# Transposing a stack of 32x32 blocks as one compact 128-partition tile, with ScalarE gathering and scattering

## The chip, the cores and the metric

The kernel runs on one core of a Trainium2 chip. The metric is the device time of one execution in microseconds (us). The time before is the median of three runs, 3059.33 us (3055.2 to 3061.43).

## The reference

A decoder trunk of two layers (SEQ 1024, D_MODEL 1024, float32). Each layer projects the input, runs three kinds of heads side by side (4 stick-breaking attention heads, 4 latent attention heads, 8 RWKV-7 heads), adds the result through a layer norm, and ends with a gated convolutional feed-forward block. The part that matters here is the recurrence of the RWKV-7 heads:

```python
def step(state, inp):
    r_t, w_t, k_t, v_t, kk_t, a_t = inp
    sa = jnp.einsum('bhvk,bhk->bhv', state, -kk_t)
    state = (state * w_t[:, :, None, :] + sa[..., None] * (kk_t * a_t)[:, :, None, :]
             + v_t[..., None] * k_t[:, :, None, :])
    return state, jnp.einsum('bhvk,bhk->bhv', state, r_t)
```

The kernel does not run it token by token. It cuts the 1024 tokens into 16 chunks of 64. Inside a chunk, each token's `sa` depends on the earlier tokens of the chunk through a strictly triangular 64x64 matrix, so that every chunk of every head needs the inverse of (identity minus that matrix).

## The kernel before, in words

The program is one long list of instructions per engine. The engines are TensorE (PE), VectorE (DVE), ScalarE (ACT), GpSimd (POOL), and SyncE (SP), which issues every DMA. A scheduler has put the instructions of all stages in one order, by priorities and by its own model of the durations. Each engine then runs its own list strictly in that order, and waits at an instruction whose inputs are not ready while everything behind it waits too.

Each of the two layers has these stages: projections and preparation of the RWKV heads (`proj_rw`, `rw_prep`, `rw_stage1`), the inversion (`rw_inv`), the walk over the chunks (`rw_chain`), the two kinds of attention, the output projection, and the feed-forward block. `rw_inv` runs twice in a layer (`st` 0 and 1, four heads each), so four times in the program. It is a generator: `phase_a` advances it between projections (`step`), so that its instructions lie among those of other stages. The first inversion of a layer lies among the projections, preparation and `rw_stage1` of the next heads; the second lies among the chunk walk of the first four heads and the projections of stick-breaking attention.

One call of `rw_inv` inverts 64 matrices of 64x64. `Aa` holds them: four heads by 16 chunks in the free dimension, two chunks side by side in the partition halves. The diagonal 32x32 blocks are first transposed into `LA` (line 725, four instructions of 32 partitions each, one per group of 32 partitions). VectorE inverts them by forward substitution, many small multiplications (line 729, product into the scratch tile `pd`) and sums (line 730, result into `T`). `T` is then transposed as a whole into `LA` (line 750, a tile of 128 partitions), TensorE forms the products with the off-diagonal blocks (line 759, evicted by ScalarE at line 762 into the buffer of `pd`), GpSimd clears the whole of `Aa` (line 764), and VectorE transposes `T` back into the diagonal blocks of `Aa`, now called `Z` (line 767, four instructions of 32 partitions). TensorE makes the off-diagonal block of the inverse (line 776, evicted at 779) and applies the inverse to `xt` (line 788, evicted at 789). `xt` is loaded from DRAM by SyncE (line 784) into the buffers of `LA` and `T`, and stored to `psd` (line 792), from which `rw_chain` loads it (line 831).

`LA`, `T` and `pd` have one buffer each: a new tile of a name waits until every reader of the old one is done.

Names that the text uses around it: `psmm` are the projections' matrix products (lines 205 to 207, 24 for each half of 512 tokens); lines 596 and 597 are two matmuls that sum over a head, whose inputs come from ScalarE (line 200) and VectorE (line 201); lines 844 to 847 make the matrices `QC` of the chunk walk (matmul, VectorE additions, ScalarE copy); lines 863 and 866 carry its state.

Of the kernel before, what the change touches and what calls it, by code (L numbers as in the profile page):

```python
# [17 lines left out]
P = 128  # L18
S = 1024
# [50 lines left out]
class Body:  # L70
# [640 lines left out]
    def rw_inv(self, st, tp, Aa):  # L711
        nc = self.nc
        v32 = lambda t: t.rearrange("p (a b) -> p a b", b=32)
        LA = v32(self.t(tp, [P, S], "LA"))
        T = v32(self.t(tp, [P, S], "T"))
        pd = self.t(tp, [P, S], "pd")
        M = self.t(tp, [P, 16, 16], "M")
        nc.gpsimd.memset(T, 0.0)
        Tf = T.rearrange("p a b -> p (a b)")
        nc.gpsimd.memset(Tf[:, 0:1024:33], 1.0)  # L720
        Af = Aa.rearrange("p h (j e) x -> p (h j) e x", e=2)
        for q in range(4):
            r = slice(32 * q, 32 * q + 32)
            x0 = 32 * (q % 2)
            nc.vector.transpose(LA[r], Af[r, :, q // 2, x0 : x0 + 32].rearrange("p f t -> p t f"))  # L725
            if q % 2:
                yield
        blk = lambda ap, off, dims: bass.AP(tensor=ap.tensor, offset=ap.offset + off, ap=[list(ap.ap[0])] + [list(d) for d in dims])
        mul = lambda o, x, y: nc.vector.tensor_tensor(o, x, y, op=ALU.mult)  # L729
        red = lambda o, x: nc.vector.tensor_reduce(o, x, axis=AX.X, op=ALU.add)  # L730
        for t in range(1, 16):
            pr = pd[:, : 2 * t * t].rearrange("p (b j i) -> p b j i", b=2, j=t)
            mul(pr, blk(LA, t * 32, [[528, 2], [0, t], [1, t]]), blk(T, 0, [[528, 2], [1, t], [32, t]]))
            red(blk(T, t * 32, [[528, 2], [1, t]]), pr)
            if t % 3 == 0:
                yield
        for j0 in range(0, 16, 4):
            ni = 16 - j0
            pr = pd[:, : 16 * 4 * ni].rearrange("p (t j i) -> p t j i", t=16, j=4)
            mul(pr, blk(LA, 512 + j0, [[32, 16], [0, 4], [1, ni]]), blk(T, j0 * 32 + j0, [[0, 16], [1, 4], [32, ni]]))  # L740
            red(M[:, :, j0 : j0 + 4], pr)
            yield
        for t0 in range(0, 16, 4):
            ni = t0 + 4
            pr = pd[:, : 4 * 16 * ni].rearrange("p (t j i) -> p t j i", t=4, j=16)
            mul(pr, blk(T, (16 + t0) * 32 + 16, [[32, 4], [0, 16], [1, ni]]), blk(M, 0, [[0, 4], [1, 16], [16, ni]]))
            red(blk(T, (16 + t0) * 32, [[32, 4], [1, 16]]), pr)
            yield
        T11 = LA
        nc.vector.transpose(T11.rearrange("p f j -> p j f"), T.rearrange("p t j -> p j t"))  # L750
        M1 = v32(self.t(tp, [P, S], "pd"))
        for m in range(2):
            fs = slice(16 * m, 16 * m + 16)
            psM = self.pst("pi").rearrange("p (f j) -> p f j", j=32)
            for f in range(16):
                for e in range(2):
                    r = slice(64 * e, 64 * e + 32)
                    r2 = slice(64 * e + 32, 64 * e + 64)
                    nc.tensor.matmul(psM[r2, f, :], Af[r, 16 * m + f, e, 32:64], T11[r, 16 * m + f, :], start=True, stop=True)
            for e in range(2):  # L760
                r2 = slice(64 * e + 32, 64 * e + 64)
                nc.scalar.copy(M1[r2, fs], psM[r2])
        Z = Aa.rearrange("p h (j e) x -> p (h j) (e x)", e=2)
        nc.gpsimd.memset(Z, 0.0)
        for q in range(4):
            r = slice(32 * q, 32 * q + 32)
            nc.vector.transpose(Z[r, :, 32 * q : 32 * q + 32].rearrange("p f t -> p t f"), T[r])  # L767
        yield
        for m in range(2):
            fs = slice(16 * m, 16 * m + 16)  # L770
            psZ = self.pst("pi").rearrange("p (f j) -> p f j", j=32)
            for f in range(16):
                for e in range(2):
                    r = slice(64 * e, 64 * e + 32)
                    r2 = slice(64 * e + 32, 64 * e + 64)
                    nc.tensor.matmul(psZ[r, f, :], M1[r2, 16 * m + f, :], Z[r2, 16 * m + f, 64 * e + 32 : 64 * e + 64], start=True, stop=True)
            for e in range(2):
                r = slice(64 * e, 64 * e + 32)
                nc.scalar.copy(Z[r, fs, 64 * e + 32 : 64 * e + 64], psZ[r])
            yield  # L780
            for h in range(2):
                hd = 2 * (3 - m if st else m) + h
                xt = self.t(tp, [P, S], ("LA", "T")[h]).rearrange("p (j x) -> p j x", x=P)
                nc.sync.dma_start(xt, self.xxd[:, :, hd].rearrange("j p x -> p j x"))
                for g in range(2):
                    pP = self.pst("pi").rearrange("p (j x) -> p j x", x=P)
                    for jj in range(4):
                        nc.tensor.matmul(pP[:, jj, :], Z[:, 16 * m + 8 * h + 4 * g + jj, :], xt[:, 4 * g + jj, :], start=True, stop=True)  # L788
                    nc.scalar.copy(xt[:, 4 * g : 4 * g + 4], pP)
                for e in range(2):  # L790
                    er = slice(64 * e, 64 * e + 64)
                    nc.sync.dma_start(self.psd[:, er, hd, e, :].rearrange("j p x -> p j x"), xt[er])
                yield
# [460 lines left out]
```

## Time and profile before

| | |
|---|---|
| median of three runs | 3059.33 us (3055.2 to 3061.43) |
| the profiled execution's own time | 3062.54 us |
| its span, first to last instruction | 3060.8 us |
| PE busy | 2941.1 us (96%) |
| PEld (weight loads, beside PE) | 2342.6 us (77%) |
| DVE busy | 1774.8 us (58%) |
| ACT busy | 1045.0 us (34%) |
| POOL busy | 234.2 us (8%) |
| TensorE's mean granted clock | 0.98 |

The profiled execution is one execution; its time lies 3.2 us above the median of the runs. The 1.7 us between its time and its span lie before the first and behind the last instruction. Busy shares are means over stages that differ: the feed-forward stages take half of the span with PE at 99%, while the inversions lie in four short stretches, about 219 to 300 us and 349 to 465 us in the first layer, and 1742 to 1825 us and 1874 to 1990 us in the second.

### The profile page before, as it was taken

To read this page: it belongs to the slowest core of one execution; us is meant where nothing else is said; L and a number is where in the kernel's file an instruction comes from. 1 tells how busy PE (TensorE), PEld (TensorE's weight loads), DVE (VectorE), ACT (ScalarE), POOL (GpSimd) and SP (SyncE) were. 2 spreads that over 40 slices of the span, in tenths; PEclk is the share of its full clock that TensorE was granted. 3 is DMA by queue.
4 is the path that set the end of the run, shared out by engine and by line. 5 is a ranking of instruction groups with operands and counts; after the bars stand their busy time and mean duration, and the time that the engine had idled before them with its cause. 6 is when DMAs were issued, how large, how long until landed. Compare 5 with 4: busy or idle time off the path is not lost.

```text
span 3060.8 us, 41867 instructions
## 1 busy us (share of the span) xinstructions
PE 2941.1 (96%) x16572; PEld 2342.6 (77%) x16572; DVE 1774.8 (58%) x2881; ACT 1045.0 (34%) x1801; POOL 234.2 (8%) x308
## 2 busy tenths in 40 slices
PE   8999999989999999999999999999899999999998
PEld 6766777766888888888877677776678888888887
DVE  4579764886644444444645787658865444444436
ACT  5454443763221112121244543447622111212120
POOL 0001121131000000000000011210300000000000
PEclk9999999899999999999999999999999999999999
DMA  4353656324421111111124446563244111111111
GB/s 132 94 153 107 196 178 202 104 59 138 166 62 56 42 42 49 55 49 56 59 80 112 133 121 202 168 206 93 82 134 165 55 42 42 48 55 49 55 49 55
DMA packets 338259, 301.78 MB, mean 99 GB/s; under 512 B 24200, under 2 KB 302992, under 8 KB 338064
## 3 DMA queue, kind: packets, MB, share of 16 engines
q1 hardware_dynamic: 338064, 299.11, 32.3%
q8 instruction: 131, 2.15, 0.3%
q14 instruction: 64, 0.52, 0.1%
HBM read 208.87 MB, written 90.18 MB: 98 GB/s over the span
## 4 chain that ended last, share of the span: by engine, by line
PE 74%; DVE 11%; issue 8%; ACT 3%; DMA 2%; POOL 1%; SPq 0%; POOLq 0%; DVEq 0%; ACTq 0%
PE psmm L205 16%; PE psmm L206 16%; PE psmm L207 16%; PE psps L205 5%; PE psps L206 5%; PE psps L207 5%; PE pspa L844 1%; DVE pd L729 1%; DVE LA L725 1%; PE pspi L788 1%; PE psmt L216 1%; DVE Aa L767 1%; DVE T L730 1%; PE pspa L684 0%; PE pspy L871 0%
## 5 line engine op out<-in xcount | busy, mean ns | idle before, releaser
L206 PE MATMUL psmm<-xTl,whi 128*128 128x512 f32 x2144 | 851.0, 397 | 0.0
L205 PE MATMUL psmm<-xTh,whi 128*128 128x512 f32 x2144 | 850.4, 397 | 0.0
L207 PE MATMUL psmm<-xTh,wlo 128*128 128x512 f32 x2144 | 848.0, 396 | 0.0
L200 ACT CAST whi<-raw 128x1024 fp32r<-128x1024 f32 x152 | 160.3, 1055 | 1059.5 <-PE psmm L206 1043.0
L205 PEld LDWEIGHTS psmm<-xTh,whi 128*128 128x128 f32 x2144 | 405.1, 189 | 89.0 <-issue 5.4
L207 PEld LDWEIGHTS psmm<-xTh,wlo 128*128 128x128 f32 x2144 | 405.3, 189 | 87.9 <-issue 4.2
L206 PEld LDWEIGHTS psmm<-xTl,whi 128*128 128x128 f32 x2144 | 405.3, 189 | 87.9 <-issue 4.4
L201 DVE TENSOR_TENSOR wlo<-raw,whi 128x1024 fp32r<-128x1024 f32 x152 | 185.5, 1220 | 465.3 <-ACT whi L200 447.9
L1056 DVE TENSOR_TENSOR y<-y,psps 128x512 f32<-128x512 f32 x288 | 196.3, 686 | 171.4 <-PE psps L207 171.3
L205 PE MATMUL psps<-wdh,hh 128*128 128x512 f32 x672 | 266.8, 397 | 0.0
L206 PE MATMUL psps<-wdl,hh 128*128 128x512 f32 x672 | 262.9, 391 | 0.0
L207 PE MATMUL psps<-wdh,hl 128*128 128x512 f32 x672 | 259.7, 391 | 0.0
L205 PEld LDWEIGHTS psps<-wdh,hh 128*128 128x128 f32 x672 | 126.1, 188 | 36.8 <-ACT hh L200 6.0
L919 POOL TENSOR_TENSOR lsm<-lsm,small 128x1 f32<-128x1 f32 x32 | 29.0, 905 | 1634.0 <-DVE lsm L918 1634.0
L207 PEld LDWEIGHTS psps<-wdh,hl 128*128 128x128 f32 x672 | 126.2, 188 | 26.9
L206 PEld LDWEIGHTS psps<-wdl,hh 128*128 128x128 f32 x672 | 126.2, 188 | 25.3
L1031 DVE TENSOR_TENSOR cv<-cv,psmm 128x1024 f32<-128x1024 f32 x44 | 53.7, 1221 | 136.1 <-PE psmm L207 131.1
L201 DVE TENSOR_TENSOR wdl<-raw,wdh 128x1024 fp32r<-128x1024 f32 x42 | 51.5, 1225 | 88.6 <-ACT wdh L200 88.6
L1026 ACT ACTIVATE cv<-cv 128x1024 f32<-128x1024 f32 x44 | 46.8, 1063 | 116.0 <-DVE cv L1025 116.0
L844 PE MATMUL pspa<-RBl,PSl 128*128 128x128 f32 x512 | 73.6, 291 | 11.9 <-ACT QC L847 8.9
L844 PEld LDWEIGHTS pspa<-RBl,PSl 128*128 128x128 f32 x512 | 66.5, 200 | 19.5 <-ACT QC L847 10.8
L206 PE MATMUL psmm<-wol,whi 128*128 128x512 f32 x192 | 76.9, 401 | 2.0 <-DVE wol L201 2.0
(442 smaller groups left out, 4568.2 us busy)
## 6 DMA issues: line engine op xcount, KB each, us to landing
raw<-in_ffn_w_up_dram SPq DMA_DIRECT2D x88, 512.0 KB
raw<-in_w_in_dram SPq DMA_DIRECT2D x44, 512.0 KB
raw<-in_ffn_w_down_dram SPq DMA_DIRECT2D x44, 512.0 KB
rbd<-RB SPq DMA_DIRECT2D x64, 256.0 KB
PSl<-psd SPq DMA_DIRECT2D x32, 512.0 KB
RBl<-rbd SPq DMA_DIRECT2D x32, 512.0 KB
psd<-Vz SPq DMA_DIRECT2D x64, 128.0 KB
xxd<-X SPq DMA_DIRECT2D x64, 128.0 KB
```

The costliest lines, as they stand in the source:

```text
L200: self.nc.scalar.copy(hi, src)
L201: (eng or self.nc.vector).tensor_tensor(lo, src, hi.bitcast(F32), op=ALU.subtract)
L205: mm(out, lh, rh, start=start, stop=False)
L206: mm(out, lh, rl, start=False, stop=False)
L207: mm(out, ll, rh, start=False, stop=stop)
L216: nc.tensor.transpose(pt[:, k * P : k * P + P], xt[:, kk * P : kk * P + P], self.ident)
L725: nc.vector.transpose(LA[r], Af[r, :, q // 2, x0 : x0 + 32].rearrange("p f t -> p t f"))
L729: mul = lambda o, x, y: nc.vector.tensor_tensor(o, x, y, op=ALU.mult)
L844: nc.tensor.matmul(pQ[:, f, e, :], PSh[:, f, h, e, :], RBh[:, f, h, e, :], start=True, stop=True)
L1026: nc.scalar.activation(cv, cv, AF.Gelu)
L1031: nc.vector.tensor_tensor(cv, cv, pg, op=ALU.mult)
L1056: nc.vector.tensor_tensor(y[:, i, hs], y[:, i, hs], ps, op=ALU.add)
```

## The change

The four transpositions of 32 partitions at either end of the inversion become one transposition of 128 partitions each. For this the diagonal blocks are first copied by ScalarE into a compact tile (`pd`, four copies of 32 partitions), and the transposed result goes to a compact tile `zt` (a new tile in the buffer of `LA`), from which ScalarE copies it into the diagonal blocks of `Z` (four copies).

```diff
@@ -714,6 +714,7 @@
         pd = self.t(tp, [P, S], "pd")
+        pd3 = v32(pd)
         M = self.t(tp, [P, 16, 16], "M")
@@ -722,9 +723,10 @@
         for q in range(4):
             r = slice(32 * q, 32 * q + 32)
             x0 = 32 * (q % 2)
-            nc.vector.transpose(LA[r], Af[r, :, q // 2, x0 : x0 + 32].rearrange("p f t -> p t f"))
+            nc.scalar.copy(pd3[r], Af[r, :, q // 2, x0 : x0 + 32])
             if q % 2:
                 yield
+        nc.vector.transpose(LA, pd3.rearrange("p f t -> p t f"))
@@ -762,9 +764,11 @@
         nc.gpsimd.memset(Z, 0.0)
+        zt = v32(self.t(tp, [P, S], "LA"))
+        nc.vector.transpose(zt.rearrange("p f t -> p t f"), T)
         for q in range(4):
             r = slice(32 * q, 32 * q + 32)
-            nc.vector.transpose(Z[r, :, 32 * q : 32 * q + 32].rearrange("p f t -> p t f"), T[r])
+            nc.scalar.copy(Z[r, :, 32 * q : 32 * q + 32], zt[r])
         yield
```

Lines of the changed kernel behind this place are numbered higher: the copies are lines 726 and 771, the transpositions 729 and 768; 729 and 730 of before are 731 and 732, 784 is 788 and 792 is 796.

The scheduler makes a new order of all engines from it. Three places show how. In all rows, the number behind a name is that of the buffer's tile.

On VectorE at the first inversion of the first layer, the order before goes from the last mask products of `rw_stage1` (689, 690) to the transpositions, and then to `q` for the sums over a head (201):

```order
L689 TENSOR_TENSOR Aa_878<-pspy_1823,maskA_98 128x256
L690 TENSOR_TENSOR RB_1806<-pspy_1823,maskA_98 128x4x64
L725 STREAM_TRANSPOSE LA_1918<-Aa_878 32x1024 x4
L201 TENSOR_TENSOR q_352_1978<-kk_1954,q_351_1977 128x512
L729 TENSOR_TENSOR pd_1920<-LA_1918,T_1919 128x2
L201 TENSOR_TENSOR q_355_1986<-kk_1954,q_354_1985 128x512
```

Now, on the same engine at the same place, where 633 and 634 are the decay's addition and running sum for one half of the tokens:

```order
L689 TENSOR_TENSOR Aa_878<-pspy_1823,maskA_98 128x256
L690 TENSOR_TENSOR RB_1806<-pspy_1823,maskA_98 128x4x64
L633 TENSOR_SCALAR tw_1953<-tw_1953 128x512
L634 SCALAR_TENSOR_TENSOR tw_1953<-m_18_104,tw_1953 128x512
L729 STREAM_TRANSPOSE LA_1918<-pd_1920 128x1024
L633 TENSOR_SCALAR tw_1953<-tw_1953 128x512
L731 TENSOR_TENSOR pd_1920<-LA_1918,T_1919 128x2
L634 SCALAR_TENSOR_TENSOR tw_1953<-m_18_104,tw_1953 128x512
L732 TENSOR_REDUCE T_1919<-pd_1920 128x2
L201 TENSOR_TENSOR q_352_1979<-kk_1955,q_351_1978 128x512
```

One half of the decay's sum has moved ahead of the transposition, and `q` has moved behind the other half. On TensorE, the first sum over a head (596) now stands 17 projection matmuls later, and the second (597) still follows it closely.

On ScalarE at the same place, the four copies now stand between the evictions of `rw_prep` (611); before, no row stood between 700 and the second 611:

```order
L611 ACTIVATE tw_1953<-pspq_1956,small_15_95 128x512
L700 COPY X_1807<-pspa_1836 128x2x64 x2
L726 COPY pd_1920<-Aa_878 32x1024 x4
L611 ACTIVATE tw_1953<-pspa_1961,small_15_95 128x512
L611 ACTIVATE ta_1954<-pspy_1966,small_15_95 128x512
L611 ACTIVATE ta_1954<-pspa_1971,small_15_95 128x512
L200 CAST q_351_1978<-kk_1955 128x512
```

The three evictions and the cast have moved behind the copies.

On VectorE at the second inversion of the first layer, before (`sg` is the gate's projection, `wlo` the low part of a weight tile):

```order
L689 TENSOR_TENSOR Aa_878<-pspy_3066,maskA_98 128x256
L690 TENSOR_TENSOR RB_3049<-pspy_3066,maskA_98 128x4x64
L725 STREAM_TRANSPOSE LA_3272<-Aa_878 32x1024 x4
L201 TENSOR_TENSOR wlo_4139<-raw_4137,whi_4138 128x1024
L308 TENSOR_TENSOR sg_3117<-sg_3117,small_15_95 128x1
L311 SCALAR_TENSOR_TENSOR sg_3117<-psmm_3146,pv_67_288,sg_3117 128x511
L729 TENSOR_TENSOR pd_3274<-LA_3272,T_3273 128x2
```

And now:

```order
L308 TENSOR_TENSOR sg_3120<-sg_3120,small_15_95 128x1
L311 SCALAR_TENSOR_TENSOR sg_3120<-psmm_3149,pv_67_288,sg_3120 128x511
L689 TENSOR_TENSOR Aa_878<-pspa_3068,maskA_98 128x256
L690 TENSOR_TENSOR RB_3052<-pspa_3068,maskA_98 128x4x64
L689 TENSOR_TENSOR Aa_878<-pspy_3069,maskA_98 128x256
L690 TENSOR_TENSOR RB_3052<-pspy_3069,maskA_98 128x4x64
L729 STREAM_TRANSPOSE LA_3275<-pd_3277 128x1024
L731 TENSOR_TENSOR pd_3277<-LA_3275,T_3276 128x2
```

The gate's two rows have moved ahead of the last mask products. A `wlo` (201) has gone from here; the next one now stands inside the substitution, ten steps on and ahead of the first `QC` addition.

On SyncE at the end of the first inversion, the loads of `xt` have changed places. Before, `LA` is loaded first and `T` three rows later:

```order
L784 DMA LA_2255<-xxd_121 128x8x128
L659 DMA bvd_124<-q_414_2513 128x4x128
L709 DMA psd_122<-Vz_181_876 64x4x128 x3
L784 DMA T_2271<-xxd_121 128x8x128
L704 DMA rbd_120<-RB_2516 128x2x256 x2
```

Now `T` comes first, and a weight tile (239) stands behind the load of `LA`:

```order
L788 DMA T_2274<-xxd_121 128x8x128
L788 DMA LA_2258<-xxd_121 128x8x128
L659 DMA bvd_124<-q_415_2516 128x4x128
L239 DMA raw_4143<-in_w_in_dram 128x8x128
L704 DMA rbd_120<-RB_2519 128x2x256
```

Further on, the order of TensorE in the first layer's attention has changed in about a hundred places; in the second layer's attention it has not.

## Rows read from the trace of the kernel before

**Rows 1.** The page: busy time of each engine.

```profile
PE 2941.1 (96%) x16572; PEld 2342.6 (77%) x16572; DVE 1774.8 (58%) x2881; ACT 1045.0 (34%) x1801; POOL 234.2 (8%) x308
```

**Rows 2.** Busy time by stretch (from:to, length, engines, clock, DMA share, GB/s).

```profile
140.00:220.00 80.00, 76.35 (x521) 55.88 (x519) 54.12 (x113) 40.88 (x85) 4.86 (x9) 0.98 0.47 138
220.00:300.00 80.00, 70.64 (x560) 53.68 (x559) 76.96 (x124) 34.41 (x63) 8.09 (x7) 0.98 0.36 102
345.00:445.00 100.00, 92.65 (x807) 73.98 (x806) 80.81 (x149) 34.96 (x68) 13.81 (x12) 0.93 0.60 190
...
1740.00:1820.00 80.00, 72.33 (x543) 54.07 (x541) 77.05 (x127) 33.48 (x59) 10.90 (x7) 0.93 0.35 97
```

**Rows 3.** VectorE's groups by shape, 215 to 445 us (busy, mean ns, idle before).

```profile
L725 DVE STREAM_TRANSPOSE LA<-Aa 32x1024 f32<-32x1024 f32 x8 | 15.9, 1987 | 0.1
L767 DVE STREAM_TRANSPOSE Aa<-T 32x1024 f32<-32x1024 f32 x8 | 15.7, 1957 | 1.2 <-POOL Aa L764 1.0
L201 DVE TENSOR_TENSOR wlo<-raw,whi 128x1024 fp32r<-128x1024 f32 x10 | 12.2, 1218 | 2.1 <-PE psmm L207 2.1
...
L750 DVE STREAM_TRANSPOSE LA<-T 128x1024 f32<-128x1024 f32 x2 | 4.3, 2134 | 0.0
```

**Rows 4.** ScalarE's groups by shape, 215 to 445 us.

```profile
L200 ACT CAST whi<-raw 128x1024 fp32r<-128x1024 f32 x9 | 9.4, 1049 | 11.3 <-PE psmm L206 9.6 <-issue 1.7
...
L762 ACT COPY pd<-pspi 32x512 f32<-32x512 f32 x8 | 4.6, 580 | 2.1 <-PE pspi L759 2.0
```

**Rows 5.** Timeline of the first transpositions, 215 to 233 us (start, us, instruction, idle before).

```profile
219.40 7.88 DVE L725 STREAM_TRANSPOSE LA<-Aa 32x1024 f32<-32x1024 f32 x4
...
228.06 0.50 PE L597 MATMUL pspq<-q,bonesr 128*128 128x512 f32 x1 [2.14 <-DVE q L201]
...
229.48 0.63 PE L206 MATMUL psmm<-xTl,whi 128*128 128x512 f32 x1
...
232.97 0.40 PE L206 MATMUL psmm<-xTl,whi 128*128 128x512 f32 x1
```

**Rows 6.** TensorE's waits, 215 to 345 us: total, times, longest.

```profile
PE pspi L776 <- DVE Aa L767: 2.3, 2, 1.5
```

**Rows 7.** Timeline of the second inversion's start, 345 to 376 us.

```profile
349.03 8.10 DVE L725 STREAM_TRANSPOSE LA<-Aa 32x1024 f32<-32x1024 f32 x4
...
359.03 0.15 DVE L729 TENSOR_TENSOR pd<-LA,T 128x2 f32<-128x2 f32 x1
...
369.33 0.41 DVE L845 TENSOR_TENSOR QC<-pspa,arl 64x256 f32<-64x256 f32 x1
...
370.86 2.08 PE L844 MATMUL pspa<-RBl,PSl 128*128 128x128 f32 x8 [3.80 <-ACT QC L847]
```

**Rows 8.** Timeline of the first inversion's end, 276 to 300 us.

```profile
282.99 0.36 SPq L784 DMA_DIRECT2D LA<-xxd  x1
283.03 3.52 POOL L764 MEMSET Aa<- 128x4096 f32 x1 [16.06 <-PE pspi L759]
...
287.06 7.84 DVE L767 STREAM_TRANSPOSE Aa<-T 32x1024 f32<-32x1024 f32 x4
...
297.87 1.05 PE L788 MATMUL pspi<-LA,Aa 128*128 128x128 f32 x8
```

**Rows 9.** The chain that ended last, 460 to 480 us (start, us, what).

```profile
460.37 0.23 PE psmm L206
...
471.03 4.71 DMA PSl<-psd
```

**Rows 10.** The same chain over the span: the end of the walk, and attention.

```profile
502.86 1.98 PE pspa L844 x16
...
601.71 10.24 issue
...
2027.36 1.98 PE pspa L844 x16
...
2120.06 10.22 issue
```

## The prediction, made blind

> **What bounds the kernel now.** I read the page first. TensorE is busy for 2941.1 us [rows 1] of a span of 3060.8 us, so all that any change outside TensorE can win back is the 119.7 us in which it idles, plus what it loses at the lower clock. VectorE's 1774.8 us look harmless as a mean, so the next question is where the changed instructions stand.
>
> The stretches answer it [rows 2]. From 220 to 300 us, where the first inversion lies, VectorE is busy for 76.96 of 80 us, and TensorE idles for 80 - 70.64 = 9.36 us. In the 80 us just ahead, which have the same projections and the same `rw_stage1` but no inversion, VectorE has only 54.12 us to do and TensorE idles for 3.65 us. So the first inversion makes VectorE the bound for some 80 us. The second layer repeats this: VectorE 77.05 us, TensorE idle 7.67 us. Around the second inversion (345 to 445 us) VectorE is busy for 80.81 of 100 us and TensorE idles for 7.35 us.
>
> The groups by shape then price the instructions [rows 3, 4], and the timelines show who waits for them. After the first four transpositions of 32 partitions, 7.88 us in one piece, TensorE stands for 2.14 us at line 597, because its input `q` (line 201) was queued behind them on VectorE. [...]
>
> **The change, part by part.** VectorE is relieved. At the first end, 4 x 1.987 = 7.95 us become one transposition of 128 partitions. The trace has that very shape in line 750: 2.13 us [rows 3]. At the other end 4 x 1.957 = 7.83 us become 2.13 us as well. That is 5.8 + 5.7 = 11.5 us for each inversion and 46 us for four.
>
> [...]
>
> ScalarE takes on eight copies of 32 partitions by 1024 elements for each inversion. No row has one, and there are two sides to its price. A cast of 128 partitions by 1024 from SBUF to SBUF takes 1.05 us; a copy of 32 partitions by 512 takes 0.58 us, half of the width for a little over half of the time, so fewer partitions bring nothing [rows 4]. The other bound is a transposition of the same strided shape, 1.99 us [rows 3]. I take 1.05 us, since it is the same engine, so 4.2 us for each set of four.
>
> Place one, `LA` of the first inversion. The copies wait for the same last mask product as the transpositions did, and ScalarE is free at about 220.5 us. They end at 224.7, the transposition at 226.9; before, `LA` was ready at 227.28. So the substitution starts only 0.4 us earlier: VectorE, which takes its list in order, stands at the new transposition for about 3 us, with `q` and the substitution behind it. Of the 5.8 us freed here only what the new order puts ahead of it is used, one half of the decay's sum, 1.6 us. But TensorE now has 17 projection matmuls more ahead of line 596, at 0.23 us each in the chain [rows 9] 3.9 us of cover. `q` (201) comes at about 229.5 us, and TensorE reaches 597 at about 229.2. So the stop of 2.14 us goes, and with it seven matmuls of 0.63 instead of 0.40 us, 1.6 us. I count 3.7 us.
>
> Place two, the end of the first inversion. GpSimd's clearing ends at 286.55 us, and VectorE's four transpositions run from 287.06 to 294.90 [rows 8]. Now the transposition into `zt` needs only `T`, and the buffer of `LA`, free after line 759 at 282.95. It is hidden under the clearing, and the four copies follow from about 286.6 to 290.8 us: the diagonal is complete 4.1 us sooner. That removes the 2.3 us that TensorE waits at line 776 [rows 6]. Against it stands a new wait. `xt` is loaded into the buffer of `LA`, at 282.99 us before [rows 8]; now the load must wait for the copies out of `zt`. The nearest row for 512 KB is 4.71 us [rows 9], so it lands 0.4 + 4.7 = 5.1 us after the diagonal is complete, while line 788 started 3.0 us after that before. TensorE has other rows between 776 and 788 and might stand for 1 to 2 us; the bounds are nothing and 2.1 us plus those rows. I take 1.1, so 1.2 us are won here.
>
> Behind the waiting load on SyncE stand `bvd` and a weight tile. Before, the queue stood at the load of `T` until the transpositions were done, so it is freed sooner now, and this costs nothing.
>
> The first inversion thus gives 4.9 us for each layer. The stretches check it: if TensorE's idle time falls to that of the stretch without an inversion, 9.36 - 3.65 = 5.7 us in the first layer and 7.67 - 3.65 = 4.0 in the second, 4.85 on average.
>
> Place three, the second inversion. The gate's two rows now stand ahead of the last mask products and delay them by 0.9 us. The copies then run to about 354.3 us, the transposition to 356.5, and the substitution starts at about 356.5 instead of 359.03 [rows 7]. But a weight subtraction of 1.22 us and a sum of 0.56 now stand ahead of the `QC` addition (845), so it comes at about 368.6 instead of 369.33, and of TensorE's 3.80 us stop at line 844 only 0.7 go. At the far end, four transpositions no longer lie between the `QC` and state instructions of the chunk walk. I take half of the 2.8 us that TensorE waits there (776 and 863), less 0.6 for the new load of `xt`. Together 1.5 us for each layer.
>
> ScalarE's other work is pushed back: behind the gathers stand the evictions of line 611, behind the scatters, which wait for GpSimd's clearing, the evictions of 306 and 779 and the `QC` copies of 847. In 220 to 300 us ScalarE is busy for 34.41 of 80 us [rows 2], so 8.4 us fit, and three `psmm` buffers let TensorE run on. If that cover fails, each set costs up to 4.2 us; I count 0.3 for each of four, 1.3 in all.
>
> The sum: 2 x 4.9 + 2 x 1.5 - 1.3 = 11.5 us. From the profiled execution's own 3062.5 us that gives 3051.0; it lies 3.2 us above the median of the runs, so I predict 3048 us for the median.
>
> **The rivals.**
>
> *The relief is spent waiting.* VectorE stands for ScalarE at four places, TensorE stands for the load of `xt`, and the stops only move. For it: the substitution starts just 0.4 us earlier at place one. Then 4 x (1.2 to 2) us of place one's clock and place two's wait go to new stops, and 2 to 4 us remain: 3056 us. Also here belongs a bad turn of the first layer's attention, whose order the scheduler has changed. How much order alone is worth there shows between the layers: from the end of the walk to the same point of attention it takes 601.71 - 502.86 = 98.9 us in the first, and 2120.06 - 2027.36 = 92.7 us in the second [rows 10]. So about 6 us, either way, which I count at nothing in the sum.
>
> *The strided copies are slow.* If ScalarE needs as long as VectorE's strided transposition, 1.99 us, place one takes 4 x 1.99 + 2.13 = 10.1 instead of 7.9 us, and the end of the inversion 8.0 instead of 7.8 us with the load of `xt` 5 us behind it. With 2.2 + 2.2 us later in each inversion, where VectorE idles instead of working, none of the gains remain and four times 4.4 us are lost: 3059 + 18 = 3077 us. It decides from 1.44 us for a copy, where 4 copies and a transposition equal 7.88 us. Against it: ScalarE's rows go by the width alone.
>
> *All of TensorE's idle time in the four stretches goes*, down to that of the stretch ahead of them: 9.7 us from the first inversions and 2 x (7.35 - 2) from the second, with the clock as well, 22 us: 3037 us.
>
> **How the numbers follow.** My forecast has 0.50, the relief spent waiting or undone by attention's order 0.27, slow copies or another loss of more than 6 us 0.15, and nearly all of the idle time 0.08. Differences of 0.2%, 6.1 us, are about what these runs can tell from no change. Faster by more has the forecast and the full gain, 0.58; within it 0.27; slower 0.15. The range goes from the full gain, 3037 us, to 3064 us, where a loss of 5 us by attention's order is taken in; below lie 0.07 and above 0.13. The forecast's own range is 3041 to 3053 us.
>
> **What would show it.** In the changed profile: transpositions of 128 partitions near 2.13 us, copies near 1.05 us; VectorE's total down by about 46 us and ScalarE's up by about 34; the stop at 597 after the first transposition gone; TensorE's idle time in the 80 us around the first inversions near 4.5 us; a stop at the first line 788 of an inversion of 1 to 2 us. I am wrong if the copies take over 1.44 us, if TensorE's stop at 788 is 3 us or more, if ScalarE's queue makes TensorE wait where it did not, or if the first layer's attention is 6 us longer.

## The result, and the profile after

The changed kernel takes 3025.17 us (median of 4 runs, 3022.94 to 3027.41) against 3057.26 us (the kernel before, with a fourth run): a ratio of 0.9892, 95% interval 0.9880 to 0.9905. That is 32 us faster, where 11.5 were forecast and 3037 us was the low end of the range. The profiled execution took 3025.69 us, its span 3024.0. In the kernel after, lines 759, 776 and 844 of before are 761, 780 and 848, and 788 is 792. Below, "gather" is the copies ahead of the substitution, "scatter" those behind it.

The page's busy line answers [rows 1]:

```profile
PE 2913.1 (96%) x16572; PEld 2322.0 (77%) x16572; DVE 1727.8 (57%) x2857; ACT 1074.8 (36%) x1833; POOL 230.8 (8%) x308
```

VectorE lost 47.0 us and ScalarE gained 29.8, near the 46 and 34 forecast. In these two executions TensorE's idle time (span less busy) fell only from 119.7 to 110.9 us, by 8.8. The other 28.0 us of the span are TensorE being *busy* for less time with the same products: it ran faster, at a mean granted clock of 0.989 instead of 0.980.

That pair overstates the clock. The profiled execution of the kernel before had a mean granted clock of 0.980, while 60 other runs of that kernel have 0.981 to 0.987. The profiled executions of e5 and e10 below, which leave VectorE and ScalarE the old work and take as long as the kernel before, idle for 121.2 and 120.2 us and are busy for 2927.6 and 2929.9 us. In the runs taken beside e16 the granted clock is 0.984 on average for the kernel before (nine runs) and 0.989 for the changed one (four): what is missing to 1.00, times the time, an estimate of what the clock costs, is 49 and 34 us. So about 15 of the 30 us gained there, half, are clock, and 9 to 12 us are idle time.

The groups by shape (215 to 445 us; busy, mean ns, idle before) show the prices, and VectorE's waits (total, times, longest) the new stop:

```profile
L729 DVE STREAM_TRANSPOSE LA<-pd 128x1024 f32<-128x1024 f32 x2 | 4.2, 2123 | 7.5 <-ACT pd L726 7.5
...
L768 DVE STREAM_TRANSPOSE LA<-T 128x1024 f32<-128x1024 f32 x2 | 4.1, 2064 | 1.8 <-PE pspi L761 1.8
```

```profile
L726 ACT COPY pd<-Aa 32x1024 f32<-32x1024 f32 x8 | 8.4, 1044 | 0.5 <-DVE Aa L689 0.4
L771 ACT COPY Aa<-LA 32x1024 f32<-32x1024 f32 x8 | 8.3, 1042 | 0.2
```

```profile
DVE LA L729 <- ACT pd L726: 15.0, 4, 4.5
```

2.1 us for a transposition and 1.04 us for a copy are what was forecast (2.13 and 1.05). VectorE stands 15.0 us in all for the gather, 3.8 us on average; about 3 were forecast for the first. The stretches answer [rows 2], where 1717 to 1797 us now stands for 1740 to 1820 before. The last three are cut by the program's own marks, the first at the first product of line 761 (759 before), which takes the transposed `T`, called T11 in the kernel:

```profile
220.00:300.00 80.00, 74.85 (x636) 58.42 (x636) 65.00 (x117) 42.98 (x72) 8.16 (x7) 0.98 0.37 103
345.00:445.00 100.00, 95.72 (x937) 76.69 (x937) 71.53 (x153) 47.83 (x85) 20.40 (x20) 0.98 0.66 204
1717.00:1797.00 80.00, 73.49 (x571) 56.22 (x569) 68.63 (x124) 42.81 (x68) 8.12 (x7) 0.98 0.36 104
274.80:410.70 135.90, 130.68 (x1139) 101.00 (x1139) 97.40 (x200) 69.26 (x127) 19.41 (x29) 0.99 0.66 199
410.70:455.30 44.60, 43.74 (x543) 36.47 (x543) 17.85 (x43) 26.25 (x47) 13.65 (x14) 1.00 0.58 174
455.30:513.20 57.90, 54.24 (x460) 44.60 (x459) 29.91 (x83) 22.07 (x43) 11.00 (x12) 1.00 0.70 224
```

The same three program stretches of the first layer before the change, from the first inversion's T11 products to the second's, to the last product of the second inversion, to attention's first score product:

```profile
278.80:414.30 135.50, 126.36 (x1105) 98.58 (x1105) 106.30 (x198) 59.48 (x113) 18.58 (x29) 0.97 0.63 191
414.30:465.70 51.40, 49.00 (x550) 41.04 (x550) 23.59 (x46) 21.18 (x42) 13.44 (x14) 0.93 0.53 154
465.70:529.90 64.20, 60.56 (x476) 48.10 (x476) 31.14 (x84) 23.30 (x45) 10.97 (x12) 1.00 0.65 207
```

Read them together. The three take 251.1 us before and 238.4 after, 12.7 us less. TensorE idles (length less busy) for 9.14 + 2.40 + 3.64 = 15.2 us before, 5.22 + 0.86 + 3.66 = 9.7 after: 5.4 us. The granted clock was 0.97 and 0.93, and is 0.99 and 1.00: what is missing to 1.00 times the length is 4.1 + 3.6 us before and 1.4 after, 6.3 us. (These shares are rounded; the two traces show granted clocks of 1.00 and 0.50 only, and the lower level, 0.50, for 13.7 us of the three stretches before and 3.4 after; half of the difference, by the same estimate, is 5.1 us.) The middle stretch shows it best: 6.8 us shorter, of which 3.6 are clock and 1.5 idle time. The rest is work that went elsewhere, as the projection products alone (tile psmm) in the same stretches show, before and after:

```profile
278.80:414.30 135.50, 66.79 (x241) 0.97 0.63 191
414.30:465.70 51.40, 19.99 (x74) 0.93 0.53 154
465.70:529.90 64.20, 28.00 (x99) 1.00 0.65 207
```

```profile
274.80:410.70 135.90, 72.50 (x259) 0.99 0.66 199
410.70:455.30 44.60, 18.70 (x67) 1.00 0.58 174
455.30:513.20 57.90, 22.45 (x83) 1.00 0.70 224
```

The first stretch is no shorter than before, but does 18 projection products more, 4.1 us at 0.23 each [rows 9]; the two behind it do 23 fewer. A stretch's length alone would have put the gain in the wrong place.

What stood at the end of the second inversion before (TensorE's timeline, 429 to 438 us: start, us, instruction, idle before):

```profile
430.19 0.22 PE L776 MATMUL pspi<-Aa,pd 32*32 32x32 f32 x2 [0.67 <-DVE Aa L767]
...
436.01 0.57 PE L776 MATMUL pspi<-Aa,pd 32*32 32x32 f32 x24 [1.08 <-DVE Aa L767]
436.63 0.33 PE L863 MATMUL pspy<-S,QC 128*64 128x64 f32 x2
...
437.56 0.47 PE L863 MATMUL pspy<-S,QC 128*64 128x64 f32 x2
```

VectorE had taken the four transpositions one by one between `QC` additions, from 425.64 to 435.96 us. Two stops of 0.67 and 1.08 us follow, and then the same two products of line 863 take 0.47 us instead of 0.33: the granted clock is 0.50 for 6.8 us from 437.3. Afterwards the transposition runs beside GpSimd's clearing (418.18 to 421.71 us), and the products of line 780 start without a stop:

```profile
418.16 2.03 DVE L768 STREAM_TRANSPOSE LA<-T 128x1024 f32<-128x1024 f32 x1 [0.76 <-PE pspi L761]
```

```profile
426.91 0.24 PE L780 MATMUL pspi<-Aa,pd 32*32 32x32 f32 x2
...
429.89 1.19 PE L780 MATMUL pspi<-Aa,pd 32*32 32x32 f32 x62
```

Over the whole span of these two executions, TensorE was at the lower level, 0.50, for 123.5 us before and 71.2 after; half of the difference, 26 us, is time by the same estimate. In e5's execution, with the old transpositions, it was 93.5 us, so that part of this difference is the execution and not the change.

### The profile page after: what moved, and what is told of

Its sections match the earlier page's. It is cut to its first block, busy times and chain, and to the rows that moved or that the text cites. A ratio compares the mean times of both kernels' runs of the same rounds, so it can differ in the third digit from the quotient of the medians.

```text
span 3024.0 us, 41845 instructions
## 1 busy us (share of the span) xinstructions
PE 2913.1 (96%) x16572; PEld 2322.0 (77%) x16572; DVE 1727.8 (57%) x2857; ACT 1074.8 (36%) x1833; POOL 230.8 (8%) x308
## 4 chain that ended last, share of the span: by engine, by line
PE 76%; DVE 10%; issue 8%; ACT 3%; DMA 3%; POOL 1%; SPq 0%; POOLq 0%; DVEq 0%; ACTq 0%
PE psmm L207 16%; PE psmm L206 16%; PE psmm L205 16%; PE psps L205 5%; PE psps L206 5%; PE psps L207 5%; PE pspa L848 2%; DVE pd L731 1%; PE pspi L792 1%; PE psmt L216 1%; DMA LA<-xxd 1%; DVE T L732 1%; PE pspa L684 1%; ACT pd L726 0%; DVE mexp L400 0%
```

## The experiments

Ratios are to the kernel before on the same chip, with their 95% intervals; the changed kernel was run again beside e13 to e15, as e16 (0.9905).

| run | what | us | ratio |
|---|---|---|---|
| e1 | scatter end only | 3044.1 | 0.9963 (0.9951 to 0.9976) |
| e2 | gather end only | 3042.1 | 0.9956 (0.9938 to 0.9973) |
| e3 | change, transpositions in four pieces | 3047.1 | 0.9972 (0.9960 to 0.9984) |
| e4 | change, `xt` buffers exchanged | 3030.3 | 0.9921 (0.9906 to 0.9936) |
| e5 | before, another order | 3054.1 | 1.0005 (0.9994 to 1.0015) |
| e6 | scatter end only, in four pieces | 3046.6 | 0.9977 (0.9965 to 0.9989) |
| e7 | change, copies twice | 3053.6 | 0.9998 (0.9987 to 1.0009) |
| e8 | change, gather in twelve pieces | 3025.8 | 0.9910 (0.9895 to 0.9925) |
| e9 | second inversion only | 3028.6 | 0.9912 (0.9897 to 0.9927) |
| e10 | before, clearing around the diagonal | 3056.0 | 1.0001 (0.9991 to 1.0010) |
| e11 | change, clearing around the diagonal | 3036.0 | 0.9938 (0.9918 to 0.9957) |
| e12 | change, gather shared with GpSimd | 3030.1 | 0.9915 (0.9901 to 0.9930) |
| e13 | first inversion only | 3043.4 | 0.9960 (0.9947 to 0.9974) |
| e14 | second, and gather of the first | 3031.7 | 0.9933 (0.9916 to 0.9949) |
| e15 | second, and scatter of the first | 3023.1 | 0.9900 (0.9885 to 0.9915) |
| e16 | the change again | 3026.0 | 0.9905 (0.9890 to 0.9920) |

**Each end alone (e1, e2).** e1 keeps the four old transpositions into `LA`, e2 the four old ones into `Z`.

> Only the end of the inversion is changed (T transposed at once into zt, ScalarE scatters); LA is made by four VectorE transpositions as before. The order of the first layer's attention on TensorE is that of the kernel before, word for word. Theory A (VectorE's relief at the end of the second inversion is what pays: the stops at the psZ products of the inversion go and with them 6.8 us at the lower clock behind them): the stretch from the end of the substitution of the second inversion to the start of the second chunk walk is 6 to 8 us shorter in each layer, the first inversion about 1 us, the attention of the first layer 0: about 3041 us, 16 us under the kernel before. Rival B (what pays is mainly another order of walk and attention that the change brought by chance): less than 8 us under the kernel before, 3050 us or more. The step as predicted (2.7 us for each layer at these places) would give 3052 us.

> Only the start of the inversion is changed (ScalarE gathers, one transposition); the end has its four VectorE transpositions as before. The order of the first layer's attention is here that of the changed kernel. Theory A: the stops at lines 597 and 596 go (2 to 4 us in each layer), the 6 to 8 us at the end of the second inversion do not come, the attention of the first layer is about 9 us shorter as in the changed kernel: about 3042 us. Rival B: the order of attention and walk brings nearly all of the gain here: 3030 us or less. If relief alone counted and attention's 9 us belonged to the end of the inversion: 3050 us.

e2 has theory A's time (3042.1 us, 13 under the kernel before), but not its terms: attention's new order is worth some 3.5 us (see e5), not 9. e1's 11 us (interval 7 to 15) lie between theory A's 16 and rival B's 8, and its trace decides for theory A's place. From the T11 products of the second inversion to its last product, e1 takes 45.9 us at a clock of 1.00; e2 still has 48.5 us at 0.93:

```profile
409.20:455.10 45.90, 44.77 (x546) 37.27 (x539) 18.53 (x42) 25.00 (x47) 13.26 (x14) 1.00 0.58 171
```

```profile
412.80:461.30 48.50, 45.84 (x494) 37.69 (x487) 21.55 (x38) 21.23 (x41) 12.22 (x13) 0.93 0.54 157
```

So the stop and the clock there belong to the scatter end. The traces of all runs agree. The five kernels that keep the old transpositions at the end of the second inversion (before, e2, e5, e10, e13) have 3.4 to 6.8 us at the lower level in this stretch, in both layers; of the thirteen others only e3 has any, 6.8 us in its second layer.

**Shorter, or hidden? (e3, e6, e10).** Copies and buffers stay as in the change (e6: at the end only), but VectorE does each transposition in four pieces (the scatter end's is shown, the other is alike):

```diff
-        nc.vector.transpose(zt.rearrange("p f t -> p t f"), T)
+        for q in range(4):
+            r = slice(32 * q, 32 * q + 32)
+            nc.vector.transpose(zt[r].rearrange("p f t -> p t f"), T[r])
```

e10 is the kernel before, with GpSimd clearing only what lies beside the diagonal blocks:

```diff
-        nc.gpsimd.memset(Z, 0.0)
+        for q in range(4):
+            r = slice(32 * q, 32 * q + 32)
+            for o0, o1 in ((0, 32 * q), (32 * q + 32, P)):
+                if o1 > o0:
+                    nc.gpsimd.memset(Z[r, :, o0:o1], 0.0)
```

> The whole change with its ScalarE copies, but each of the two transpositions made in four pieces of 32 partitions, as long as before (about 2 us each), so VectorE gets no relief and ScalarE keeps the added copies. Theory A: VectorE's relief is the cause, so the gain at the inversions goes and the copies' wait of some 3 us each comes on top: the stretches around the inversions are as long as before or 2 to 4 us longer in each; with 9 us from attention's order (which is that of the changed kernel) about 3052 us, and 3060 without. Rival B (order): within 6 us of the changed kernel, 3031 us or less.

> The end of the inversion alone, as in the run with only that end, but T is transposed into zt in four pieces of 32 partitions: VectorE does as much as before, yet hidden under GpSimd's clearing, since the pieces need only T, and ScalarE scatters. If it is the hiding under the clearing that pays at the end of the second inversion: from the T11 products to the last product of the inversion 45 to 47 us instead of 51.4, total within 3 us of the run with only that end, about 0.3 to 0.4% under the kernel before. If VectorE's shorter time pays: 50 to 51 us there, and the total within 3 us of the kernel before.

> The kernel before with one thing changed: GpSimd clears only the blocks beside the diagonal (in seven pieces, some 10.5 us estimated from 4096 columns in 3.52 us, instead of 3.52), so VectorE's four transpositions into Z wait no longer for the clearing. VectorE's and ScalarE's work is that of the kernel before. If the wait for the clearing is what the end of the inversion lost: 45 to 47 us instead of 51.4 from the T11 products to the last product of the second inversion, and 3044 to 3048 us. If VectorE's 7.8 us count: 51 us there and within 4 us of the kernel before. If the longer clearing holds up line 788: slower than the kernel before.

With VectorE as long at work as before, and waiting for the copies besides, e3 keeps 9 of the change's 29 to 33 us, with attention nearly in the new order: the shorter work is most of the cause. For the end of the inversion taken by itself it is the place instead: e6 gains 7 us where e1 gains 11 (0.9977 and 0.9963, intervals overlapping), and its second inversion ends without a stop at line 776 and at a clock of 1.00, since its pieces need only `T`:

```profile
418.70:464.80 46.10, 44.19 (x548) 36.78 (x541) 25.34 (x51) 27.21 (x50) 14.31 (x15) 1.00 0.60 182
```

The 46.1 us prove nothing by themselves. In e5, with the old transpositions in another order, this stretch is as long, with 29 matmuls fewer in it than in the kernel before; but e5 has the stop at line 776 (1.9 us) and the lower clock:

```profile
413.40:459.50 46.10, 44.04 (x521) 37.05 (x521) 21.55 (x40) 20.44 (x41) 12.35 (x13) 0.96 0.56 163
```

e10 has the time of the kernel before. Its transpositions still write the buffer that the products of line 759 read, and so still come behind these; from 277 to 460 us TensorE waits at line 780 (776 before) almost as long as at both ends before, 2.3 [rows 6] and 1.7 us:

```profile
PE pspi L780 <- DVE Aa L771: 3.6, 2, 2.3
```

Not waiting for the clearing did not remove this stop. But e10 is no clean test of the total: its clearing takes 10.8 us instead of 3.5, and VectorE's waits for the walk's sum `mo` on GpSimd grow from 16.9 to 26.8 us over the span (more under e11). That a buffer of its own, `zt`, is what lets the transposition start sooner is argued from this order; no run changes the buffer alone. For the gather no run tells shorter and earlier apart.

**Order alone (e5).** One memset more changes the scheduler's order of the walk in some 100 places:

```diff
         nc.gpsimd.memset(T, 0.0)
+        nc.gpsimd.memset(M[:, 0, 0:1], 0.0)
```

> Order alone: the kernel before with one GpSimd memset of one element per partition more in the inversion (into M, which is written later anyway). No work worth a number is added, but the scheduler's order of the walk changes in about 100 places, and 4 to 5 of some 240 projection matmuls move; the attention's order stays. Theory A (relief and hidden waits are what paid): within 4 us of the kernel before. Rival B (another order is worth up to 9 us by chance): 6 us or more from it, on either side.

Nothing, so rival B falls for the walk's order. Attention's order is worth more: from attention's first score product to the layer's last feed-forward product the first layer takes 1005.0 to 1005.7 us in the three traces with the new order (the change, e2, e16), and 1007.6 to 1010.6 in the thirteen with the old one, on average 3.5 us more. (e3 and e7, nearly in the new order, have 1005.3 and 1004.0.)

**ScalarE's copies (e7).**

```diff
-            nc.scalar.copy(pd3[r], Af[r, :, q // 2, x0 : x0 + 32])
+            for _ in range(2):
+                nc.scalar.copy(pd3[r], Af[r, :, q // 2, x0 : x0 + 32])
...
-            nc.scalar.copy(Z[r, :, 32 * q : 32 * q + 32], zt[r])
+            for _ in range(2):
+                nc.scalar.copy(Z[r, :, 32 * q : 32 * q + 32], zt[r])
```

> The whole change with each of ScalarE's copies made twice, one after the other: 2.09 us instead of 1.04 for each block, 8.3 us more on ScalarE for an inversion, and VectorE waits 4.2 us longer for the gather. The rival of slow copies as it was predicted: with 1.99 us a copy nothing of the gain remains and four times 4.4 us are lost, 3077 us, 50 above the changed kernel. Theory A (TensorE has projection matmuls to do under these waits, as the scheduler puts more of them there): 2 to 4 us for an inversion, 3033 to 3041 us.

Between the two: 28 us above the change, 7 for an inversion, 0.84 us for each us of ScalarE's. TensorE's longest waits in 215 to 345 us are now for `q` behind VectorE's longer stand, and for the load of `xt` behind the copies:

```profile
PE pspy L668 <- DVE q L644: 3.9, 1, 3.9
PE pspi L794 <- DMA LA<-xxd: 2.7, 1, 2.7
```

So copies of twice the length are on the path, and all of the gain would be gone at about 2.1 us a copy, not at the predicted 1.44. The reverse does not follow, as the next runs show.

**Less waiting for the gather (e8, e12).** e8 copies in three steps, those of the feature tile that is ready first ahead (`p4` and `A5` are views of `pd3` and `Aa` with the tile and pair apart); e12 gives half of the copies to GpSimd.

```diff
+        ho, hn = (slice(2, 4), slice(0, 2)) if st else (slice(0, 2), slice(2, 4))
+        for hs, js in ((ho, slice(0, 8)), (hn, slice(0, 4)), (hn, slice(4, 8))):
+            for q in range(4):
...
+                nc.scalar.copy(p4[r, hs, js], A5[r, hs, js, q // 2, x0 : x0 + 32])
```

```diff
-            nc.scalar.copy(pd3[r], Af[r, :, q // 2, x0 : x0 + 32])
+            (nc.scalar.copy if q % 2 else nc.gpsimd.tensor_copy)(pd3[r], Af[r, :, q // 2, x0 : x0 + 32])
```

> The gather in twelve pieces instead of four: what the first of the two feature tiles wrote (half of the columns) and the first half of the second are copied as soon as they are masked, so that after the last mask product four copies of 32x256 remain (estimated 0.35 us each, worked out from 32x512 in 0.58) instead of four of 32x1024 at 1.04. Theory A: VectorE's wait for the gather, 15.0 us in all in the changed kernel, falls to 4 to 8 us, and TensorE's stop of 3.6 us at line 676 with the 3.4 us at the lower clock behind it goes or halves in each layer: 3 to 5 us less for each, 3016 to 3020 us. Against it stands that the first layer's attention has the order of the kernel before again, up to 3 us. Rival: VectorE's list is in order and the stop only moves to the next row, so no gain: 3024 to 3030 us.

> The whole change with two of the four gathering copies on GpSimd, beside ScalarE's two. If a GpSimd copy of 32x1024 takes 1 to 2 us, the gather ends after 2 to 4 us instead of 4.2, VectorE's wait of 15.0 us in all for the gather falls to 6 to 14 us, and 1 to 2 us for an inversion are won: 3017 to 3024 us. Rival, as the split gather showed: a shorter wait of VectorE at this place gives TensorE nothing, and the time stays within 4 us of the changed kernel, 3021 to 3029 us; if GpSimd's copies take over 3 us it is slower, 3030 us or more.

VectorE's 15.0 us of waiting fell to 0.8 and 0.5 us, as the waits of e8 and e12 show, and neither kernel is faster than the change:

```profile
DVE LA L733 <- ACT pd L730: 0.8, 2, 0.4
```

```profile
DVE LA L729 <- ACT pd L726: 0.5, 2, 0.3
```

The times alone do not decide, since both kernels have the old order of attention and so lack its 3.5 us. The traces of the first layer do: the first T11 product follows 53.7 and 54.0 us after the last mask product, 56.9 in the change, yet attention's first score product comes 295.1 and 295.8 us after it, as in the change and e16 (295.2 and 296.1); in the second layer 293.2 and 294.7 against 295.5 and 294.8. So the rival was right: ending VectorE's wait for the gather gains at most about 2 us a layer, and in the first nothing. In e8 TensorE still stops for 2.1 us at line 676, where the change has 3.6.

**The load of xt, and the clearing (e4, e11).** e4 exchanges the buffers, e11 adds e10's edit to the change.

```diff
-                xt = self.t(tp, [P, S], ("LA", "T")[h]).rearrange("p (j x) -> p j x", x=P)
+                xt = self.t(tp, [P, S], ("T", "LA")[h]).rearrange("p (j x) -> p j x", x=P)
```

> The whole change, but the first load of xt goes into the buffer of T, which is free as soon as the transposition into zt is done, and the second into that of LA (zt). Theory A: TensorE's wait at line 792 for the load (0.9 us in the first layer, 2.0 in the second) goes: 2 to 4 us less at the inversions. The order of the first layer's attention turns back to that of the kernel before; if that order is what makes the 9 us between the walk and attention of the first layer, these are lost: about 3031 us in all; if they come from VectorE's relief, 3022 us. Rival: the wait at 792 moves on to the second load (line 792 with T before): 3025 us, same.

> The whole change with the same clearing around the diagonal blocks, so ScalarE's four copies wait no longer for GpSimd. Theory A (stops at lines 780 and 792 are what is left): the diagonal is complete up to 3.5 us sooner, but most of this stop is gone already: 0 to 3 us under the changed kernel, 3022 to 3026 us. Rival: the clearing of some 10.5 us ends after the copies and holds up the products with xt at line 792: 3 to 8 us for each inversion, 3037 to 3057 us.

In e4's second layer TensorE's wait for the load around the first inversion falls from 1.4 to 0.2 us, yet the kernel is some 5 us slower than the change (3030.3 us against 3025.2 and 3026.0). The old order of attention, to which it turns back, accounts for some 3.5 of these. Besides, its trace has 10.2 us at the lower clock from 1782 us, behind three stops (3.67, 0.68 and 0.50 us) that the changed kernel has at the same places (3.62, 0.66 and 0.48 us), with a granted clock of 1.00 behind the last two (1770 to 1790 us). Why, stays open. e11 is 10 us slower than the change, at another place than its rival said; it too has the old order of attention. The clearing in six pieces takes 10.8 us on GpSimd (2.66, 1.80 and 0.94 us, two of each, in e10), and behind it stands the walk's sum `mo` (line 908, here 912). VectorE waits for it 14.2 us in 405 to 450 us, where the change waits 5.1 in the like stretch:

```profile
DVE mo L913 <- POOL mo L912: 14.2, 4, 11.6
```

**The two inversions (e9, e13, e14, e15).** Each edit is the change under a condition on the inversion, here the gather's in e9 (`not st` in e13; the scatter's likewise):

```diff
+            if st:
                 nc.scalar.copy(pd3[r], Af[r, :, q // 2, x0 : x0 + 32])
+            else:
+                nc.vector.transpose(LA[r], Af[r, :, q // 2, x0 : x0 + 32].rearrange("p f t -> p t f"))
```

> Both ends of the inversion are changed, but only in the second inversion of each layer; the first keeps its eight VectorE transpositions. This prices what the prediction called place three, at 1.5 us for each layer with 0.6 for ScalarE's queue off. As predicted: 2 to 3 us in all, 3052 us, same as before. Theory A (the end of the second inversion alone gives 5 us with its clock, its start and the walk 3 to 5 more): 8 to 10 us for each layer, 3035 to 3039 us. Rival: what the second inversion gained came from matmuls that the first one's relief let through, so the second alone gives 2 to 4 us for each: 3047 to 3051 us.

> Both ends of the inversion are changed, but only in the first inversion of each layer. As predicted for places one and two, 4.9 us for each layer: 9 to 10 us, 0.3% under the kernel before. If the first inversion's gain is given back at the second (whose stops are those of the kernel before): 0 to 4 us, same. If the two inversions' gains add up to that of the whole change, whose share is 1.08% against 0.88% for the second alone: 0.2%, 6 us.

> The gather in both inversions, the scatter in the second only. If the start of the first inversion (place one, predicted 3.7 us for each layer) pays by itself: 5 to 8 us under the second inversion alone, so 0.2% under it and level with the whole change. If it is given back: within 3 us of the second inversion alone, 0.88% under the kernel before.

> The scatter in both inversions, the gather in the second only. Place two (predicted 1.2 us for each layer): 2 to 3 us under the second inversion alone. Rival: TensorE's wait for the load of xt behind the scatter takes the place of its stop at the psZ products: within 2 us of the second alone, 0.88% under the kernel before.

> The changed kernel again, beside these: 1.0 to 1.2% under the kernel before. Theory A (clock behind the stops of the second inversion) and its rival both give this; it sets what the three others are compared with.

The second inversion alone gives 0.88%, 27 us, more than theory A said; the first alone 0.40%, 12 us. Together they would be 1.28%; the change has 0.95 to 1.08%, so 6 to 10 us are lost where both meet (the sum's own interval is about 0.2%, 6 us). e14 and e15 say where: with the second inversion changed, neither the first's gather (0.9933 against 0.9912) nor its scatter (0.9900) brings anything beyond the intervals. From the last mask product ahead of the first inversion to attention, e9 takes 296.4 and 294.6 us in the two layers, the change 295.2 and 295.5, the kernel before 310.8 and 309.2. By the granted clocks of all runs, about 12 of e9's 26 us are clock, none of e13's 12, and 8 of e15's 32. e15 runs from T11 to T11 at a clock of 1.00:

```profile
278.00:409.20 131.20, 127.97 (x1159) 100.99 (x1161) 97.32 (x204) 70.96 (x127) 21.64 (x32) 1.00 0.66 200
```

It makes four copies fewer in each layer and is level with the change (the intervals overlap), so no version was shown to beat it.

## Why the prediction was right in direction and wrong in size

**What bounds the kernel** held, with one word too little: TensorE's clock was named beside its idle time, but priced only at place one. The sum holds 8.3 us of idle time and 3.2 of clock; over the whole kernel 9 to 12 us of idle time went, and about 15 of clock.

**Place one (3.7 us a layer)** has about the right size by another way. From the last mask product to the first T11 product it takes 59.6 and 59.8 us in the two layers before, and 56.9 in both now. The stop of 2.14 us at line 597 is gone [rows 5], that at 596 too, but a stop that was not foreseen took their place, at line 676, whose `q` (653) is late on VectorE, with 3.4 us at the lower clock behind it as before (TensorE's timeline):

```profile
254.05 0.66 PE L676 MATMUL pspq<-ident,q 128*128 128x128 f32 x4 [3.61 <-DVE q L653]
```

The clock term of 1.6 us shows in the trace before at nearly its size: from 229.2 to 232.4 us the granted clock is 0.50 and the projection products start 0.43 us apart, from 232.6 to 237.0 us it is 1.00 and they start 0.23 us apart, 1.4 us for seven. And e15, which lacks the gather of the first inversion, is as fast as the change: the gather adds nothing to the rest.

**Place two (1.2 us)**: the stop at line 776 [rows 6] went, and TensorE's wait for `LA<-xxd` came, 0.9 us in the first layer and 2.0 over three waits in the second's two inversions, where 1 to 2 were predicted. The check by stretches fell short: TensorE's idle time went from 9.36 to 5.15 us in the first layer's 80 us and from 7.67 to 6.5 in the second's, 2.7 less on average, where 4.85 were counted. By itself the first inversion gives 12 us (e13), near the 9.8 of places one and two in both layers; beside a changed second inversion it gives next to nothing, so its terms do not add up with place three as the sum has it.

**Place three (1.5 us) is the term that was mis-sized.** It stands for 3 us in both layers; e9, which changes the second inversion alone, gains 27. Together with place two it stood for 2.7 us a layer; the stretches from T11 to attention measure 12.7 and, in the second layer, 10.7 us. "I take half of the 2.8 us that TensorE waits there (776 and 863)": all of the stop at 776 went. "Of TensorE's 3.80 us stop at line 844 only 0.7 go": 1.6 went [rows 7]. Above all, no clock was counted behind these stops, though the stretch's granted clock stood in the rows at 0.93 [rows 2]; it is 0.98 now. The 6.8 us at the lower level behind the second inversion's line 776 went; the 6.8 around the stop at line 844 (369.1 to 375.9 us) became 3.4, but e5 and e10, with the old gather, have 3.4 there too. Idle and clock together are 5.4 + 5.1 to 6.3 us in the first layer.

**ScalarE (-1.3 us)**: the price of 1.05 us a copy was right (1.04); the 1.3 us no run measures. The rival of slow copies put them 29 us above the forecast (3077 less 3048), and e7 is 28 us above the change. The level was wrong: the rival loses 18 us against the kernel before, while e7 is level with it, since a gain of 29 to 33 us and not of 11.5 is used up first.

**Attention's order**, counted at nothing within 6 us, gave about 3.5, a gain by luck. **The relief spent waiting** fell: VectorE's wait is real, 15.0 us, and ending it frees nearly nothing (e8, e12). **All idle time gone**, 3037 us, came nearest in number, in part by luck: it counted 20 us of idle time and 1.6 of clock.

The transposition's time is what the prediction had: 128x1024 elements take 2.06 and 2.12 us now (lines 768 and 729), 2.13 before (line 750); the subtraction of that width (line 201) takes 1.22 us [rows 3].

One profile is not exact to a few us: e5 and the kernel before have equal medians (3054.1 and 3054.4, run side by side), yet their profiled executions took 3050.55 and 3062.5 us. Shares by place above are good to some 2 us; the verdicts rest on the medians.

## What to carry to other kernels

Price a stop of TensorE with the clock behind it (here 6.8 us at 0.50 behind stops of 0.67 and 1.08 us): read the granted clock of the very stretch, and count what it lacks to 1.00 times the length beside the idle time. A stretch that gets no shorter may still have gained: count the products in it. And before shortening a wait, ask whether anyone waits behind it; removing 14 us of VectorE's here brought nearly nothing. A profile is one execution: compare the granted clock over all runs before naming its share.

## What the runs showed of the hardware

Two stops of TensorE of 0.67 and 1.08 us (0.67 and 1.07 in the second layer), some five us apart, were followed by 6.8 us at a granted clock of 0.50 in both layers of the kernel before. Equal stops can be followed by different clocks: nearly the same two (0.66 and 1.22, 0.65 and 1.24 us) by 3.4 and 6.8 us at the lower level in the two layers of e5, and e4's (the last two 0.68 and 0.50) by 10.2 us where the change (0.66 and 0.48) runs at 1.00. A ScalarE copy of 32x256 strided elements takes 0.40 us and one of 32x512 0.61 (line 730 of e8), one of 32x1024 1.04 (line 726 of the change). GpSimd's copy of 32x1024 takes as long as ScalarE's: 1.05 us (line 726 of e12).
